# Two transformer layers and two hybrid layers on one core: where the steps of a norm, a group of loads and some weight splits are issued

## The chip, the core and the metric

The kernel runs on one NeuronCore of a Trainium2 chip. Five engines work side by side, each in the order of its own queue: TensorE (PE; its weight loads are shown as PEld), VectorE (DVE), ScalarE (ACT), GpSimd (POOL) and SyncE (SP), which here only issues DMAs. The metric is the device time of one execution in microseconds (us), lower is better. Times of the kernel before: 3697.65, 3699.57 and 3701.98 us, median 3699.57.

## The reference

A stream `x` of 512 tokens by 1024 features goes through two "first" layers and two "second" layers. Weights and activations are float32. What matters here:

```python
# first block, for l in 0, 1:
y = _group_rmsnorm(mix, mix_g[l]) @ w_o[l]             # mix: four attention groups
x = _layernorm(ALPHA * x + y, ln1_g[l], ln1_b[l])
f = (silu(x @ w_gate[l]) * (x @ w_up[l])) @ w_down[l]   # d_ff 2816
x = _layernorm(ALPHA * x + f, ln2_g[l], ln2_b[l])
# second block, for l in 0, 1:
x = x + 0.5 * swiglu(rms_norm(x, ffn_norm[l, 0]), ...)
x = x + mixers(rms_norm(x, mix_norm[l]) @ w_in[l]) @ w_out[l]
x = x + 0.5 * swiglu(rms_norm(x, ffn_norm[l, 1]), ...)
```

So there are six SwiGLU feed-forward blocks (called FFN 1 to 6 here, in order of time). FFN 1 and 2 follow the output projection of the attention layers, FFN 3 follows the down projection of FFN 2, FFN 4 follows the output projection of a mixer, FFN 5 follows the down projection of FFN 4, FFN 6 follows the output projection of the second mixer.

## The kernel before, in words

**Precision.** Every float32 operand is split into a high part (a cast to float32r on ACT) and a low part (a subtraction, mostly on DVE, every other output weight on POOL), and each product is three matmuls: high-high, low-high, high-low (`mm3`). A weight is loaded by `raw` (line 255, an SP DMA into one of three `wr` buffers), and split by `weight` (line 236: cast at line 250, subtraction at line 251).

**An FFN (`swiglu`, line 705).** The hidden width is 22 tiles of 128. The first four tiles are "early": they are computed as plain products from operands that don't need the finished norm. The other 18 go in pairs through `fast` (line 604), which computes a pair of tiles with seven half-size products in place of eight, from seven combinations of `x` made by `combos` (line 564). The hidden tiles are used in three chunks (8, 8 and 6 tiles; of these 4, 2 and 3 pairs come from `fast`), each followed by eight tiles of the down projection (`dn`).

**With `finish` (FFN 1, 2, 3).** The stream still has to be normalised. `early` (line 737) multiplies the un-normalised, gain-scaled stream (`psh`, `psl`, made by `presplit`) and `unfold` (line 487) repairs the result later. Meanwhile `lnrows` gets the statistics, and its rows (`lnr`, `lnb`) are there after the second product of early tile 0. `finish` is a generator of 18 steps: 10 of the layer norm (`ln`), then 8 of `combos` (two for each of four `k`). `steps(todo, n)` in the loop over early tiles issues the next `n` of them behind early tile `f`.

**Without `finish` (FFN 4, 5, 6).** The generator is `combos` alone, 8 steps (each `k` with two scalings by a gain), issued 2 at a time behind early tiles 0, 1, 2 and the rest behind tile 3.

**The seven-product loads.** `fast` loads quarters of a pair of gate or up tiles: `e` (from quarter c), `a`, `d` and `b`, 512 KB each, on SP (line 623); and on POOL (line 621) it adds quarter `d` into `e` and quarter `c` into `a` by an accumulating DMA from DRAM. `prep(j)` splits the operand of product `j`; products 0 to 6 use a, e, e+a, b, a+c, e+a+b, d. The buffers `wr2` (five) belong to a pool that takes the place of small tiles of the attention or mixer phase; `b` uses a `wr` buffer. `fast` is called three times in each FFN, 18 times in all.

**The output projection (`project`, line 329).** For each part of the mix that is ready it issues eight jobs of `wo` weights (128x256 each for a part of two tiles) through `dense` (line 265). `dense` splits weights `AHEAD` = 3 jobs ahead of use, or the first `head` of them at once, and then into ordinary slots in place of the three `wh`/`wl` buffers. Ahead of the last part, `heads` issues gate and up of early tile 0. `last` makes the split operands of the FFN from each finished tile of `x`, and `sums` adds up its sums and squares.

**What sets the order.** Nothing is ordered by hand. A list scheduler replays the program in its own model of the chip and gives each engine the instruction that is ready there, earliest in program order first; so a DMA whose buffer is free can be issued long before the place where it is written. `tc.issue_after(ins)` keeps the instructions that a block issues on the engine of `ins` behind `ins` in that engine's queue, without waiting for it to finish.

Of the kernel before, what the change touches and what calls it, by code (L numbers as in the profile page):

```python
# [19 lines left out]
KT = 8  # L20
# [17 lines left out]
LOOK = 2  # L38
MID = 0
FIN = 0  # L40
LSTEP = 5
NSTEP = 2
SLOTF = 1
PROJ1 = dict(w=(12, 13, 14, 15), s=(8, 10), S=(9, 11), a=(0, 1), b=(2,), f=(4, 6), F=(5, 7))
# [25 lines left out]
class Ctx:  # L70
# [183 lines left out]

    def raw(self, src, n, name):
        raw = self.wp.tile([128, 1024], F32, name=self.nm(name), tag="wr", bufs=NWR)[:, :n]
        self.nc.sync.dma_start(raw, src)
        return raw

    def mm3(self, acc, l, r, first, last):  # L260
# [68 lines left out]
    def project(self, E, src, xd, parts, scale, st, mean, last, wgu):  # L329

        nc = self.nc

        def add(n, j, ps):
            x = E["x"][j]
            if n == 0 and scale != 1.0:
                nc.vector.scalar_tensor_tensor(x, x, scale, ps, op0=OP.mult, op1=OP.add)
            else:
                nc.vector.tensor_add(x, x, ps)
            if n == len(parts) - 1:
                last(x, j)  # L340
                self.sums(st, x, j, mean)
        for n in range(len(parts)):
            yield "part%d" % (n + 1)
            if n == 0:
                E["x"] = self.refill(xd)
            k, ms = parts[E["parts"][n]]
            ms = ms()
            if n == len(parts) - 1:
                self.heads(wgu)
            w = src[:, :, k * 128:(k + len(ms)) * 128]  # L350
            yield from self.dense([self.tjob(w[j], len(ms), 128, ms, lambda ps, j=j: add(n, j, ps), None, "wo")
                                   for j in range(KT)])

    def gemm(self, acc, w, xs):
        for k, x in enumerate(xs):
# [59 lines left out]
    def rows(self, col, ps=None):  # L415

        n = col.shape[-1]
        ps = self.P("rowp")[:, :n * 128] if ps is None else ps
        for t in range(n):
            self.mm(ps[:, t * 128:t * 128 + 128], col[:, t:t + 1].to_broadcast([128, 128]), self.ident)  # L420
        return ps
# [182 lines left out]
    def fast(self, wgu, f0, n, cs, rows, put, between):  # L604


        nc = self.nc
        H = KT // 2
        quarter = {"a": (0, 0), "b": (0, 1), "c": (1, 0), "d": (1, 1)}
        raws, ws = {}, {}  # L610
        total = 7 * (n // 2)

        def tile_(pool, tag, bufs, dt=F32):
            return pool.tile([128, 1024], dt, name=self.nm("sw" + tag), tag=tag, bufs=bufs)

        def move(i, q, t, add=False):
            g, h = quarter[q]
            f = f0 + 2 * i
            src = wgu[g, f:f + 2, :, h * 512:h * 512 + 512].rearrange("f p c -> p f c")
            if add:  # L620
                nc.gpsimd.dma_start(t.rearrange("p (f c) -> p f c", f=2), src, accum_op=OP.add)  # L621
            else:
                nc.sync.dma_start(t.rearrange("p (f c) -> p f c", f=2), src)

        def load(i, q, src=None):
            raws[i, q] = tile_(self.wp, "wr", NWR) if q == "b" else tile_(self.fp, "wr2", NRAW)
            move(i, src or q, raws[i, q])

        def prep(j):
            i, s = divmod(j, 7)  # L630
            R = lambda q: raws[i, q]
            if s == 0:
                if i == 0:
                    load(0, "e", "c")
                    move(0, "d", R("e"), True)
                    load(0, "a")
                load(i, "d")
                load(i, "b")
            elif s == 2:
                nc.vector.tensor_add(R("e"), R("e"), R("a"))  # L640
            elif s == 5:
                nc.vector.tensor_add(R("e"), R("e"), R("b"))
                del raws[i, "b"]
            r = R("aeebaed"[s])
            hi, lo = (tile_(self.wp, "w" + t, NWS, F32R) for t in "hl")
            nc.scalar.copy(hi, r)  # L646
            nc.vector.tensor_sub(lo, r, hi.bitcast(F32))  # L647
            ws[j] = hi, lo
            if s == 2:
                move(i, "c", R("a"), True)  # L650
            if s == 4 and i + 1 < n // 2:
                load(i + 1, "e", "c")
                move(i + 1, "d", raws[i + 1, "e"], True)
                load(i + 1, "a")
            if s >= 4:
                del raws[i, "aed"[s - 4]]
        tags = ["s", "s", "o", "d"]
        bank = 0
        acc, g, u2 = {}, {}, {}
        for j in range(min(SAHEAD, total)):  # L660
            prep(j)
        for j in range(total):
            i, s = divmod(j, 7)
            if j + SAHEAD < total:
                prep(j + SAHEAD)
            between(j)
            hi, lo = ws.pop(j)
            fresh = s in (0, 1, 3)
            if fresh:
                tag = tags[bank % 4]  # L670
                bank += 1
                acc["AE0B"[s]] = [self.P("gup", tag)[:, 0:256] for _ in range(2)]
            a = acc["AEABAEA"[s]]
            for e in range(2):
                for k in range(H):
                    w = slice(e * 512 + k * 128, e * 512 + k * 128 + 128)
                    x, first, last = cs[s][k], fresh and k == 0, k == H - 1
                    self.mm(a[e], hi[:, w], x[0], first, False, not fresh)
                    self.mm(a[e], hi[:, w], x[1], False, False, not fresh)
                    self.mm(a[e], lo[:, w], x[0], False, last, not fresh)  # L680
            A, B = slice(0, 256), slice(256, 512)
            for e in range(2):
                if s == 0:
                    g[e] = self.S("gt")
                    nc.scalar.copy(g[e][:, A], a[e])
                elif s == 1:
                    if e == 0:
                        u = self.S("up")
                        u2 = {0: u[:, A], 1: u[:, B]}
                    nc.scalar.copy(u2[e], a[e])  # L690
                elif s == 2:
                    nc.scalar.copy(g[e][:, B], a[e])
                elif s == 3:
                    nc.vector.tensor_sub(g[e][:, A], a[e], g[e][:, A])
                elif s == 4:
                    nc.vector.tensor_add(u2[e], a[e], u2[e])
                elif s == 5:
                    nc.vector.scalar_tensor_tensor(g[e][:, B], a[e], -1.0, g[e][:, B], op0=OP.mult, op1=OP.subtract)
                    if rows() is not None:
                        nc.vector.tensor_mul(g[e], g[e], rows())  # L700
                    nc.scalar.activation(g[e], g[e], AF.Silu)
                else:
                    put(f0 + 2 * i + e, g[e], a[e], u2[e])

    def swiglu(self, xs, wgu, wdn, evac, stats, ahead, finish=None, npre=0, mix=None):
# [5 lines left out]
        ws, raw, h = dict(self.head), [], [None] * FT  # L711
# [17 lines left out]
        def products(f, xs):  # L729
            w = get(f, f + 1)  # L730
            gu = [self.P("gup", "s") for _ in range(2)]
            for i in range(2):
                self.gemm(gu[i], w[i], xs)
                tick()
            return gu

        def early(f, xs):
            w = get(f, f + LOOK)
            a, out = self.P("gup", "s"), []
            for i in range(2):  # L740
                b = self.P("gux", "do"[i])[:, 0:258]
                self.gemmx(a[:, i * 256:i * 256 + 256], b, w[i], xs)
                tick()
                out.append(self.unpack(a[:, i * 256:i * 256 + 256], b, "a", "gu"[i] + "r"))
            return out
# [21 lines left out]
        def steps(it, n):  # L767
            for _ in range(n):
                try:
                    next(it)  # L770
                except StopIteration as e:
                    return True, e.value
            return False, None
        todo = None if finish else mix(cs)
        for f in range(npre):
            if finish:
                raw.append(early(f, xs))
                if f == 1:
                    lnr = rows
                    todo = finish(lnr, cs)  # L780
            else:
                raw.append([(self.evac(ps, "a", name="gu"[i] + "r"), None) for i, ps in enumerate(products(f, xs))])
            if todo:
                end, v = steps(todo, 100 if f == npre - 1 else LSTEP if finish else 2)
                if end and finish:
                    stats, ticks = v, 0
        xs = None
# [1564 lines left out]
```

## Time and profile before

| | |
|---|---|
| median of three runs | 3699.57 us |
| the profiled execution, as timed | 3712.78 us |
| its span in the profile | 3711.0 us |
| PE busy | 3561.6 us, 96% of the span |
| PEld, DVE, ACT, POOL busy | 82%, 70%, 48%, 11% |
| mean granted TensorE clock | 0.978 of full speed |
| HBM traffic | 101 GB/s over the span |

A busy engine is one with an instruction in flight. Matmuls are pipelined, so PE at 96% doesn't mean that it does 96% of what it could: a lone matmul is shown longer than the interval at which matmuls follow each other. The number of matmuls in a stretch, set against a stretch in which they run without a break, tells more. The granted clock has two levels, 1.2 and 2.4 GHz; a share of a stretch between 0.5 and 1 means that it had some of each.

### The profile page before, as it was taken

To read this page: it belongs to the slowest core of one execution; us is meant where nothing else is said; L and a number is where in the kernel's file an instruction comes from. 1 tells how busy PE (TensorE), PEld (TensorE's weight loads), DVE (VectorE), ACT (ScalarE), POOL (GpSimd) and SP (SyncE) were. 2 spreads that over 40 slices of the span, in tenths; PEclk is the share of its full clock that TensorE was granted. 3 is DMA by queue.
4 is the path that set the end of the run, shared out by engine and by line. 5 is a ranking of instruction groups with operands and counts; after the bars stand their busy time and mean duration, and the time that the engine had idled before them with its cause. 6 is when DMAs were issued, how large, how long until landed. Compare 5 with 4: busy or idle time off the path is not lost.

```text
span 3711.0 us, 58410 instructions
## 1 busy us (share of the span) xinstructions
PE 3561.6 (96%) x22612; PEld 3059.9 (82%) x22612; DVE 2611.0 (70%) x5227; ACT 1772.7 (48%) x3392; POOL 422.7 (11%) x402
## 2 busy tenths in 40 slices
PE   9998999999899999999998999999999999799999
PEld 7677989776789988889776779898989777688888
DVE  5377766747676568767699667666867678957766
ACT  5464544646454346535443645435534533445433
POOL 1112000111200010001212011000000211100000
PEclk9999999999999999999998999999999999899999
DMA  3124543221434443544211245434643321223443
GB/s 129 48 66 113 139 129 89 100 66 49 125 91 135 121 133 86 132 128 137 82 55 42 69 120 143 130 97 119 160 120 95 102 70 51 80 69 108 131 123 94
DMA packets 196998, 377.94 MB, mean 102 GB/s; under 512 B 32456, under 2 KB 58728, under 8 KB 196464
## 3 DMA queue, kind: packets, MB, share of 16 engines
q1 hardware_dynamic: 167344, 317.57, 26.5%
q0 software_dynamic: 29376, 56.63, 9.7%
q8 instruction: 178, 2.92, 0.3%
q14 instruction: 100, 0.82, 0.1%
HBM read 358.36 MB, written 15.78 MB: 101 GB/s over the span
## 4 chain that ended last, share of the span: by engine, by line
PE 74%; DVE 16%; DMA 3%; ACT 3%; issue 3%; POOL 0%; ACTq 0%; POOLq 0%; DVEq 0%; SPq 0%
PE gup L179 25%; PE dn L179 19%; PE pjp L179 6%; PE tp L179 3%; PE wop L179 3%; PE sc L179 2%; DVE swwl L647 2%; PE gux L179 2%; PE ot L179 1%; DMA swwr<-in_w_gu_dram 1%; ACT swwh L646 1%; PE pt L183 1%; PE iY L179 1%; PE G L179 1%; PE iR L179 1%
## 5 line engine op out<-in xcount | busy, mean ns | idle before, releaser
L646 ACT CAST swwh<-swwr 128x1024 fp32r<-128x1024 f32 x378 | 395.0, 1051 | 510.5 <-PE gup L179 205.3
L647 DVE TENSOR_TENSOR swwl<-swwr,swwh 128x1024 fp32r<-128x1024 f32 x378 | 460.9, 1224 | 222.5 <-ACT swwh L646 214.3
L179 PE MATMUL gup<-cth,swwh 128*128 128x256 f32 x1728 | 487.4, 284 | 21.6 <-ACT cth L592 17.3
L179 PE MATMUL gup<-cth,swwl 128*128 128x256 f32 x1728 | 488.9, 283 | 2.3 <-DVE swwl L647 2.2
L179 PE MATMUL gup<-ctl,swwh 128*128 128x256 f32 x1728 | 489.2, 283 | 1.6 <-DVE ctl L597 1.6
L179 PE MATMUL dn<-hh,downl 128*128 128x512 f32 x1056 | 413.4, 394 | 1.4 <-DVE downl L251 1.4
L179 PE MATMUL dn<-hl,downh 128*128 128x512 f32 x1056 | 414.0, 394 | 0.1
L179 PE MATMUL dn<-hh,downh 128*128 128x512 f32 x1056 | 413.1, 395 | 0.0
L179 PEld LDWEIGHTS gup<-cth,swwh 128*128 128x128 f32 x1728 | 326.5, 190 | 25.9 <-ACT cth L592 20.6
L621 POOL DMA_DIRECT2D swwr<-in_w_gu_dram x108 | 130.0, 1203 | 1862.5 <-DVE swwr L640 1068.1
L179 PEld LDWEIGHTS gup<-ctl,swwh 128*128 128x128 f32 x1728 | 328.8, 190 | 3.8 <-DVE ctl L597 3.8
L179 PEld LDWEIGHTS gup<-cth,swwl 128*128 128x128 f32 x1728 | 328.6, 190 | 3.7 <-DVE swwl L647 3.7
L250 ACT CAST downh<-down 128x1024 fp32r<-128x1024 f32 (+1 forms) x144 | 141.0, 979 | 262.0 <-PE dn L179 177.7
L179 PE MATMUL gup<-cnl,swwh 128*128 128x256 f32 x864 | 244.6, 284 | 3.0 <-DVE cnl L594 3.0
L179 PE MATMUL gup<-cnh,swwh 128*128 128x256 f32 x864 | 242.3, 284 | 2.1 <-ACT cnh L581 2.1
L179 PE MATMUL gup<-cnh,swwl 128*128 128x256 f32 x864 | 243.5, 282 | 0.0
L179 PEld LDWEIGHTS dn<-hl,downh 128*128 128x128 f32 x1056 | 198.3, 188 | 48.0 <-DVE hl L229 3.2
L179 PEld LDWEIGHTS dn<-hh,downh 128*128 128x128 f32 x1056 | 198.0, 188 | 48.3 <-ACT hh L228 2.3
L179 PEld LDWEIGHTS dn<-hh,downl 128*128 128x128 f32 x1056 | 198.3, 188 | 47.8 <-DVE downl L251 1.9
L179 PE MATMUL pjp<-xsh,pjh 128*128 128x512 f32 x472 | 202.2, 429 | 14.2 <-ACT tpe L218 8.0
L179 PE MATMUL pjp<-xsl,pjh 128*128 128x512 f32 x472 | 194.7, 413 | 3.2 <-DVE xsl L535 3.1
L179 PE MATMUL pjp<-xsh,pjl 128*128 128x512 f32 x472 | 194.5, 412 | 0.0
(649 smaller groups left out, 8666.4 us busy)
## 6 DMA issues: line engine op xcount, KB each, us to landing
swwr<-in_w_gu_dram SPq DMA_DIRECT2D x216, 512.0 KB, 4.0
swwr<-in_w_gu_dram POOLq DMA_DIRECT2D x108, 512.0 KB, 6.2
down<-in_w_dn_dram SPq DMA_DIRECT2D x96, 512.0 KB, 3.7
pj<-in_w_in_dram SPq DMA_DIRECT2D x62, 512.0 KB, 3.6
down<-in_w_dn_dram SPq DMA_DIRECT2D x48, 384.0 KB, 3.1
wo<-in_w_o_dram SPq DMA_DIRECT2D x96, 128.0 KB, 2.2
g<-in_w_gu_dram SPq DMA_DIRECT2D x24, 512.0 KB, 3.7
u<-in_w_gu_dram SPq DMA_DIRECT2D x24, 512.0 KB, 4.1
```

Source lines behind the costliest of these rows:

```text
L179: self.nc.tensor.matmul(out, l, r, start=start, stop=stop, skip_group_check=more)
L183: self.nc.tensor.transpose(out, src, self.ident if ident is None else ident)
L250: nc.scalar.copy(hi, r)
L621: nc.gpsimd.dma_start(t.rearrange("p (f c) -> p f c", f=2), src, accum_op=OP.add)
L646: nc.scalar.copy(hi, r)
L647: nc.vector.tensor_sub(lo, r, hi.bitcast(F32))
```

## The change

Three things. The steps of `finish` begin behind early tile 0 in place of tile 1, in numbers 4, 8, 6, 0 (before: none, 5, 5, the remaining 8), and those of FFN 4 to 6 in numbers 2, 4, 2, 0 (before: 2, 2, 2, 2). The first loads of each call of `fast` (`e` and `a`) are queued on SP behind the last load that `raw` has issued by then: the last early weight in the first call, the last down weight in the other two. And the last part of each output projection splits its first six weights at once, into slots.

```diff
-LSTEP = 5
+PACEF = (4, 8, 6, 0)
+PACEN = (2, 4, 2, 0)
+HLAST = 6
@@ raw
-        self.nc.sync.dma_start(raw, src)
+        self.loaded = self.nc.sync.dma_start(raw, src).ins
@@ project
             yield from self.dense([self.tjob(w[j], len(ms), 128, ms, lambda ps, j=j: add(n, j, ps), None, "wo")
-                                   for j in range(KT)])
+                                   for j in range(KT)], HLAST if n == len(parts) - 1 else 0)
@@ fast, prep
                 if i == 0:
-                    load(0, "e", "c")
+                    with self.tc.issue_after(self.loaded):
+                        load(0, "e", "c")
+                        load(0, "a")
                     move(0, "d", R("e"), True)
-                    load(0, "a")
                 load(i, "d")
                 load(i, "b")
@@ swiglu
-                if f == 1:
+                if f == 0:
                     lnr = rows
                     todo = finish(lnr, cs)
@@ swiglu
-                end, v = steps(todo, 100 if f == npre - 1 else LSTEP if finish else 2)
+                end, v = steps(todo, 100 if f == npre - 1 else PACEF[f] if finish else PACEN[f])
```

## Rows read from the trace of the kernel before

**Rows 1.** The page: the span, and the chain that ended last by engine.

```profile
span 3711.0 us, 58410 instructions
PE 74%; DVE 16%; DMA 3%; ACT 3%; issue 3%; POOL 0%; ACTq 0%; POOLq 0%; DVEq 0%; SPq 0%
```

**Rows 2.** Waits of PE: who waited for whom: us in total, times, longest.

```profile
PE gup L179 <- ACT cth L592: 17.3, 14, 2.2
PE wop L179 <- ACT woh L250: 9.0, 3, 4.5
```

**Rows 3.** Busy us (x instructions) by engine, PEclk, DMA share, GB/s: starts of `fast`.

```profile
365.00:385.00 20.00, 12.29 (x64) 9.86 (x63) 18.08 (x41) 12.15 (x28) 0.33 (x1) 0.83 0.19 26
385.00:405.00 20.00, 20.00 (x171) 20.00 (x170) 14.42 (x21) 12.87 (x19) 2.39 (x2) 1.00 0.56 136
...
1425.00:1445.00 20.00, 12.90 (x64) 11.25 (x64) 19.59 (x56) 16.24 (x34) 0.00 (x0) 0.74 0.16 26
...
2231.00:2241.00 10.00, 9.38 (x72) 8.51 (x71) 8.28 (x14) 7.99 (x16) 0.00 (x0) 1.00 0.54 121
```

**Rows 4.** Timeline of FFN 1, ACT and DVE: start, us, engine, line, operation.

```profile
331.76 0.59 ACT L510 COPY lnr<-rowp 128x512 f32<-128x512 f32 x1 [7.96 <-PE rowp L179]
...
339.74 1.28 DVE L521 TENSOR_TENSOR lnt<-x,lnr 128x512 f32<-128x512 f32 x2
...
373.17 0.41 DVE L584 TENSOR_TENSOR ct<-x 128x256 f32<-128x256 f32 x1
...
383.22 0.68 DVE L597 TENSOR_TENSOR ctl<-cu,cth 128x512 fp32r<-128x512 f32 x1
```

**Rows 5.** Busy time as in rows 3: rows ready to first `fast` product, FFN 1, 3.

```profile
332.40:366.40 34.00, 33.61 (x277) 32.95 (x276) 21.65 (x35) 15.94 (x29) 1.20 (x1) 1.00 0.17 48
...
1388.90:1424.90 36.00, 35.99 (x299) 35.51 (x298) 25.84 (x43) 20.12 (x37) 1.20 (x1) 1.00 0.14 45
```

**Rows 6.** DVE groups by line in 332.4 to 366.4: count, busy us, mean ns, idle.

```profile
L492 DVE TENSOR_TENSOR gr<-gr,lnr 128x512 f32<-128x512 f32 x4 | 2.7, 684 | 3.6 <-ACT lnr L510 3.6
```

**Rows 7.** Busy time as in rows 3: the last part of FFN 1's projection.

```profile
285.00:289.00 4.00, 3.55 (x15) 2.18 (x14) 1.83 (x4) 0.96 (x3) 0.73 (x1) 1.00 1.05 351
...
293.50:298.00 4.50, 4.50 (x11) 3.38 (x12) 1.75 (x4) 1.87 (x7) 0.72 (x1) 0.50 0.77 166
```

**Rows 8.** Timeline of ACT in that stretch: the cast of FFN 1's first up weight.

```profile
292.28 0.62 ACT L250 CAST uh<-u 128x512 fp32r<-128x512 f32 x1 [2.70 <-DMA u<-in_w_gu_dram]
```

**Rows 9.** The chain, in order of time: start, us, what (FFN 1 twice, then FFN 4).

```profile
285.06 7.20 DMA u<-in_w_gu_dram
...
402.45 6.24 DMA swwr<-in_w_gu_dram
...
2160.00 5.27 DMA wo<-in_w_o_dram
```

**Rows 10.** DMA issues: queue, count, KB each, median us from issue to landing.

```profile
swwr<-in_w_gu_dram SPq DMA_DIRECT2D x216, 512.0 KB, 4.0
swwr<-in_w_gu_dram POOLq DMA_DIRECT2D x108, 512.0 KB, 6.2
...
wo<-in_w_o_dram SPq DMA_DIRECT2D x96, 128.0 KB, 2.2
...
u<-in_w_gu_dram SPq DMA_DIRECT2D x24, 512.0 KB, 4.1
```

**Rows 11.** SP's queue in FFN 1: last early weight; last five down weights of chunk one.

```profile
324.93 0.33 SPq L257 DMA_DIRECT2D u<-in_w_gu_dram  x1
...
455.98 17.39 SPq L257 DMA_DIRECT2D down<-in_w_dn_dram  x5
```

**Rows 12.** Timeline of PE: first product of FFN 1's second call of `fast`.

```profile
503.83 0.28 PE L179 MATMUL gup<-cnh,swwh 128*128 128x256 f32 x1
```

**Rows 13.** Tile views, projection of FFN 1: count, min/median/max ns, first and last start.

```profile
L484 DVE SCALAR_TENSOR_TENSOR psl<-x,vec,psh x8: 737/1207/1784, 299.7 to 321.8; 128x512 fp32r<-128x512 f32 x8
...
L251 POOL TENSOR_TENSOR wol<-wo,woh x7: 718/740/1283, 278.2 to 311.1; 128x256 fp32r<-128x256 f32 x7
```

## The prediction

> **What bounds the kernel now.** I read the page first, for who stands on the chain that ends last: TensorE has 74% of it, DVE 16%, DMA 3%, ACT 3% [rows 1]. So a gain must come from places where PE stands still. The waits of PE name two that this change touches: its products waiting for ACT's casts of the `combos` operands, 17.3 us in 14 waits, and the output projection waiting for ACT's weight casts, 9.0 us in 3 waits [rows 2]. Both figures are too small for what is lost, because a lone matmul is shown longer than its share of a running stream and because the clock falls. The count of matmuls tells more. In the 20 us at the start of FFN 1's `fast`, 64 matmuls run; in the next 20 us, at full clock, 171 [rows 3]. 64 at that rate take 7.5 us, so 12.5 us are lost, part of it as a granted clock of 0.83. FFN 2 repeats this. FFN 3 has 64 in 20 us at a clock of 0.74, the same 12.5 us [rows 3]. FFN 4 has 72 in 10 us where 85.5 would run, a loss of 1.6 us, and FFN 5 and 6 repeat that [rows 3].
>
> Then the timeline of the stretch before it. In FFN 1 the norm's rows are ready from 331.76 on, the first norm operation on DVE starts at 339.74, and the `combos` steps run until 383.22 + 0.68 = 383.90, well past the first `fast` product at 366.4 [rows 4]. Yet between the rows and that product DVE is busy for 21.65 of 34 us, ACT for 15.94, PE without a break [rows 5]. The work that PE waits for could have been done under the early tiles; it is issued too late.
>
> **Part 1, the steps of `finish`.** Nothing is added or removed: 18 steps move forward, the norm behind tile 0, the first `combos` behind tile 1, the other three behind tile 2. Three `combos` take from 373.17 to 383.90, 3.58 us each on DVE, 14.3 us for four [rows 4]. Of DVE's 21.65 us in the window, seven `unfold` multiplies of 0.684 us (four of them in rows 6; the other three are the same operation on `up`) are 4.8 us that are written behind `fast` and can go there. The need is 21.65 - 4.8 + 14.3 = 31.2 us of 34: it fits, with 2.8 us to spare for the ping-pong between ACT and DVE [rows 5, 6]. ACT has 18 us free. In front of what does this work move? On DVE and ACT, in front of the splits of early tile 3's weights, and only with the first `combos`, 3.6 us; as the queue there has free time, I cost that at nothing, and at up to 3.6 us of PE for an FFN if it does not. I take a rest of 2.5 us of the 12.5 and so a gain of **10 us each in FFN 1 and 2** (bounds 3 and 12.5).
>
> FFN 3 has more to do: the sums of the stream and a scaling of each half by a gain. DVE: 25.84 - 4.8 + 14.3 = 35.3 of 36 us; ACT has 20.12 us, and the four `combos`, which make up most of its 16.24 us in the 20 us after, come on top, some 15 us: 35 of 36 [rows 3, 5]. Both engines are full, so the last `combos` will be some us late. I take **8 us** (bounds 2 and 12.5).
>
> FFN 4 to 6: the last `combos` moves from tile 3 to tile 2. I take 1 us of the 1.6 each, **3 us** (bounds -2, if a step delays a weight split, and 4.8).
>
> **What is late next.** With PE on time, the accumulation of quarter c into `a` follows product 2's sum and must land before product 4: a POOL DMA has a median of 6.2 us to landing [rows 10], and one stands on the chain already, 6.24 us, in FFN 1's second pair [rows 9]. In the first pair it was hidden behind the late `combos`. I give back **1.5 us in each of FFN 1 to 3, -4.5 us** (bounds 0 and -9).
>
> **Part 2, the queue of the `fast` loads.** Moved are two SP loads of 512 KB in each of 18 calls, and with the first of them POOL's accumulation into it. In FFN 1 they and what follows them are now issued inside the last part of the output projection. From 285 to 289 us the DMA engines are full, 351 GB/s [rows 7]. The first up weight, issued at 285.06, takes 7.20 us where 4.1 is the median [rows 9, 10]; ACT's queue stands behind its cast for 2.70 us [rows 8], with the output weight that PE waits for behind it; and the following 4.5 us run at a clock of 0.50 with 11 matmuls [rows 7]. Those take 0.235 us each in a full-rate stream (two of the 256-column ones of rows 3), 2.6 us, so 1.9 us go there. Gain 3.1 + 1.9 = 5.0, of which I take 4.5 in FFN 1; FFN 2 repeats the pattern with a wait one us longer, 5.0. In FFN 4 an output weight of 128 KB takes 5.27 us for a median of 2.2 [rows 9, 10], 3.1 us, and FFN 6 repeats it; 2.5 each, because the mixer's own end lies close behind. FFN 3, where down weights stand in place of output weights: 1. **Together 15.5 us** (bounds 0, if other loads of `fast` take the place of those held back, and 20).
>
> What it costs: the loads come later. In FFN 1's first call they now follow 324.93 [rows 11]; a load (4.0), an accumulation (6.2) and the splits of about 3 us are done by 340, for a product at 366. In the second call the last of the down weights is issued at 455.98 + 17.39 = 473.4 [rows 11], done by 487, for a product at 503.83 [rows 12]. 16 us and more are left, so nothing, in all 18. On POOL the moved accumulation passes the projection's sums and splits, which then start earlier, if anything.
>
> **Part 3, six weights at once.** Of the last eight output weights the splits of the fourth to sixth move ahead of the evictions of the first three jobs, with three loads of 128 KB. The same instructions run, two on POOL of 0.74 us at the median [rows 13] and one on DVE, and PE is bounded there by DVE's chain of sums and operand splits. I take 0 (bounds -2, as the first evictions come later, and 2 in each of four places).
>
> A rule bears on that. On the row: the operand split `psl` takes 0.737 us at least and 1.784 at most, 1.207 at the median [rows 13], in the stretch where POOL works on `x` and on these splits. The Trainium skill, page "SBUF — State Buffer", section "Who interferes with whom", says that a DVE instruction with two SBUF inputs and a GpSimd instruction that reads SBUF lock each other out, one waiting for the other in full. By that, two POOL splits moved out of DVE's busiest stretch would free up to 2 x 1.0 us of DVE in each of four projections, and the sum below would be 8 us better. The rows show long and short cases but not which partner made them long, so the sum goes without it.
>
> **The sum.** 10 + 10 + 8 + 3 - 4.5 + 15.5 + 0 = 42 us. The profiled execution (span 3711.0, 3712.78 with what lies around it) would become 3670.8; it is 13.2 us above the median of the runs, so against 3699.57 I forecast 3657.6, rounded to **3658 us**.
>
> **Rivals.**
> (a) The steps start earlier but the last `combos` still ends after the first product, since ACT and DVE hand each other work and the free time comes in pieces too short. For it: DVE is at 92% of the window in FFN 1 by my count and at 98% in FFN 3. Against it: before, the steps ran on DVE almost without a gap. Half of the 28 us of FFN 1 to 3: 3672 us. Chance 0.15.
> (b) The gate holds only `e` and `a`; `d` and the next pair's loads are free to go early and fill the DMA engines as before. Part 2 is then worth nothing: 3673 us. Chance 0.10.
> (c) Slower: the gate. Twelve of the 18 calls follow a chunk of the down projection, where the loads now come behind its last weight. If that weight's load is pushed back in the queue by more than the 16 us of margin, each us beyond costs PE a us, at each of twelve places. To end over 0.2% (7.4 us) slower with 42 us gained, it takes 49/12 = 4.1 us at each: loads 20 us later than now. At 5 us each, 42 - 60 = -18: 3718 us. Chance 0.07, as the down weights are paced by their three buffers and not by these loads.
> (d) It doesn't do what it says: the scheduler issues by readiness, and the norm's first steps wait for something other than their place in the program. Then parts 1 and 2 leave PE's waits as they are: 3700 us. Against it: the rows are ready 8 us before the first norm step, with DVE idle. Chance 0.07.
> (e) All of it, with the lock of DVE and POOL eased as well: 3640 us. Chance 0.03.
> The forecast itself: 0.58.
>
> **How the numbers follow.** Runs can tell a difference of about 0.2%, 7.4 us. Faster by more: forecast, a, b and e, 0.86; within: d, 0.07; slower: c, 0.07. For the range, the poor ends taken together (3 us each in FFN 1 and 2, 2 in FFN 3, 1 in FFN 4 to 6, half of part 2, less the 4.5) give a gain of 12 us, 3687; of the upper ones 12.5 x 3 + 4.8 + 20 = 62 us, 3637. From 3637 to 3687 holds the forecast and a, b, e, some 0.83 with what lies beyond the ends; c and d are left out.
>
> **What would show it.** Right, part 1: in the 20 us after FFN 1's first `fast` product some 150 matmuls, no clock below 0.9, `combos` finished on DVE within 2 us of that product; in FFN 3 some 125. Part 2: no load of `fast` on SP between FFN 1's output weights, first up weight down in about 4 us, projection and early tiles 4 to 5 us shorter. Wrong: `combos` still running 10 us after the first product; PE idle inside the early tiles for `gl` or `ul`; a wait for a `fast` load at the start of a second or third call.

## The result, and the profile after

The changed kernel takes 3664.95 us (median of 4 runs, 3659.73 to 3666.47) against 3700.78 for the kernel before (4 runs, 3697.65 to 3705.63): ratio 0.990, 95% interval 0.9882 to 0.9917, 35.8 us less. Its profiled execution took 3665.83 us. That of before, on which the prediction's rows rest, took 3712.78, 12 us over its median. So a second profile of before was taken, the **control** below, and differences of traces are taken against that.

The page after: span, chain by engine, the `fast` loads (KB each, median us to landing).

```profile
span 3664.1 us, 58412 instructions
PE 76%; DVE 15%; issue 3%; ACT 3%; DMA 2%; POOL 0%; ACTq 0%; DVEq 0%; POOLq 0%
swwr<-in_w_gu_dram SPq DMA_DIRECT2D x216, 512.0 KB, 5.4
```

The waits of PE after that answer [rows 2]: us in total, times, longest.

```profile
PE gup L181 <- ACT cth L594: 5.1, 5, 1.5
...
PE gup L181 <- ACT gr L211: 2.1, 3, 0.7
...
PE wop L181 <- ACT woh L252: 1.1, 4, 0.3
```

Both waits that the change aims at are much smaller, 17.3 to 5.1 and 9.0 to 1.1. A new one has come: PE waits 2.1 us for `gr`, ACT's evictions (copies out of the accumulator `gup` that PE has filled) of an early tile's gate product; the control's list has no such wait. The held loads now come five in a row, and the median of all 216 loads is 5.4 us instead of 4.0 [rows 10].

Busy time by window after, columns as in [rows 3] (PE, PEld, DVE, ACT, POOL, then PEclk, DMA share, GB/s): FFN 1 from the rows to the first `fast` product, the 20 us behind that product and the next 20; then the 20 us behind FFN 3's first product and the 10 us behind FFN 4's.

```profile
321.30:352.00 30.70, 30.70 (x259) 30.54 (x258) 27.20 (x52) 20.13 (x38) 1.21 (x1) 1.00 0.48 126
352.00:372.00 20.00, 16.32 (x112) 14.92 (x112) 14.03 (x27) 10.30 (x21) 1.20 (x1) 0.91 0.29 57
372.00:392.00 20.00, 20.00 (x172) 19.96 (x171) 14.31 (x20) 10.28 (x16) 2.39 (x2) 1.00 0.63 141
1386.90:1406.90 20.00, 14.78 (x71) 12.19 (x71) 16.78 (x48) 11.74 (x24) 1.20 (x1) 0.74 0.17 26
2191.00:2201.00 10.00, 10.00 (x86) 9.96 (x85) 5.14 (x5) 6.61 (x11) 0.87 (x1) 1.00 0.57 118
```

Against [rows 3], FFN 1 has 112 matmuls where 64 stood (full rate: 172), FFN 4 is at full rate with 86 for 72, and FFN 3 has hardly moved: 71 for 64, at the same clock of 0.74. The count has a catch: 24 of the 112 and 24 of the 71 are no products of `fast` but one half of early tile 3's `up` product, which before ran in front of it. Timeline of ACT and PE, FFN 1 and FFN 3:

```profile
359.94 0.36 ACT L211 COPY gr<-gup 128x256 f32<-128x256 f32 x1
360.36 0.58 PE L181 MATMUL gup<-psh,uh 128*128 128x256 f32 x1 [0.64 <-ACT gr L211]
...
1398.73 0.36 ACT L211 COPY gr<-gup 128x256 f32<-128x256 f32 x1
1399.14 0.58 PE L181 MATMUL gup<-psh,uh 128*128 128x256 f32 x1 [0.68 <-ACT gr L211]
```

These matmuls go into the accumulator that the tile's gate product fills, and wait for its eviction; ACT does that behind the last casts of the `combos`. They start 8.4 us (FFN 1) and 12.2 us (FFN 3) behind `fast`'s first product. In FFN 3, where PE had run 39 matmuls in the 12 us before, all 24 follow each other every 0.213 us at a granted clock of 0.50 (the lower level), against 0.117 us at full rate. So the first product comes earlier against its rows partly because work that stood in front of it now stands behind.

Timeline of FFN 1 after, ACT and DVE (answers [rows 4]): start, us, engine, line, operation.

```profile
321.27 0.58 ACT L512 COPY lnr<-rowp 128x512 f32<-128x512 f32 x1 [7.97 <-PE rowp L181]
...
322.49 1.28 DVE L523 TENSOR_TENSOR lnt<-x,lnr 128x512 f32<-128x512 f32 x2
...
343.92 1.05 ACT L649 CAST swwh<-swwr 128x1024 fp32r<-128x1024 f32 x1 [2.81 <-PE gup L181]
344.87 0.37 ACT L211 COPY ur<-gup 128x256 f32<-128x256 f32 x1
345.14 0.42 ACT L583 ACTIVATE cnh<-x 128x256 fp32r<-128x256 f32 x1
...
359.08 0.68 DVE L599 TENSOR_TENSOR ctl<-cu,cth 128x512 fp32r<-128x512 f32 x1
```

The norm begins 1.2 us behind the rows (from the start of ACT's copy), not 8. But the `combos` end at 359.08 + 0.68 = 359.8, still 7.8 us behind the first product at 352.0 (17.5 before). The second `combos` (345.14) follows at once on the eviction of early tile 2 (`ur`, 344.87), before which ACT had stood idle for 2.81 us: that is the place behind which it was written.

The last part of FFN 1's projection: after in two windows, and the control at the same point of the work in three (columns as above).

```profile
277.00:282.00 5.00, 4.65 (x21) 3.45 (x20) 5.00 (x10) 3.00 (x6) 1.28 (x1) 1.00 0.62 174
282.00:287.00 5.00, 3.69 (x14) 2.18 (x13) 4.04 (x6) 2.11 (x6) 0.93 (x1) 1.00 0.30 107
```

```profile
275.00:280.00 5.00, 4.55 (x19) 3.11 (x18) 3.53 (x7) 1.43 (x4) 0.17 (x1) 1.00 1.07 297
280.00:285.00 5.00, 1.74 (x6) 0.78 (x5) 2.58 (x5) 1.88 (x4) 1.78 (x2) 0.98 1.01 324
285.00:290.00 5.00, 4.71 (x14) 3.47 (x15) 2.54 (x5) 2.27 (x8) 1.03 (x1) 0.68 0.80 170
```

The full DMA engines of [rows 7] are there in the control (324 GB/s, 6 matmuls in 5 us, then a clock of 0.68) and gone after (107 GB/s, 14 matmuls, clock 1.00).

### The profile page after: what moved, and what is told of

Its sections match the earlier page's. It is cut to its first block, busy times and chain, and to the rows that moved or that the text cites. A ratio compares the mean times of both kernels' runs of the same rounds, so it can differ in the third digit from the quotient of the medians.

```text
span 3664.1 us, 58412 instructions
## 1 busy us (share of the span) xinstructions
PE 3538.9 (97%) x22612; PEld 3049.0 (83%) x22612; DVE 2616.5 (71%) x5227; ACT 1772.2 (48%) x3392; POOL 423.6 (12%) x402
## 4 chain that ended last, share of the span: by engine, by line
PE 76%; DVE 15%; issue 3%; ACT 3%; DMA 2%; POOL 0%; ACTq 0%; DVEq 0%; POOLq 0%
PE gup L181 26%; PE dn L181 19%; PE pjp L181 7%; PE wop L181 4%; PE tp L181 3%; PE sc L181 2%; DVE swwl L650 2%; PE ot L181 1%; PE gux L181 1%; DMA swwr<-in_w_gu_dram 1%; PE pt L185 1%; ACT swwh L649 1%; PE iY L181 1%; PE iR L181 1%; PE G L181 1%
```

## A ruler for the traces

For each FFN I measured one stretch: from the first matmul of its output projection to the first matmul of `fast`'s second pair of tiles (for FFN 4 and 6 from the first matmul of the projection's second part, as the first part lies inside the mixer and ends some 67 us earlier; for FFN 3 and 5, which have no projection, from the end of the FFN before). The late matmuls of early tiles lie inside it, so it holds the same work in every version but those that leave something out. It leaves out the mixers and the held loads of `fast`'s second and third calls; from its end to the end of the FFN, control and after differ by at most 1.7 us, and by 0.1 in the sum of the six. The two profiles of before differ by up to 1.1 us in a stretch and by 2.8 us in the sum: so much is scatter. In us, from the traces; the last columns are the sum of the six differences from the control, and the runs: ratio with its interval, times 3701.

| kernel | FFN 1 | FFN 2 | FFN 3 | FFN 4 | FFN 5 | FFN 6 | sum | runs |
|---|---|---|---|---|---|---|---|---|
| control | 177.6 | 178.3 | 88.0 | 124.1 | 69.0 | 121.3 | | |
| after | 166.7 | 166.2 | 85.8 | 119.0 | 66.4 | 118.5 | -35.7 | 0.9900 (-31 to -44) |
| steps alone | 170.0 | 169.1 | 86.9 | 121.6 | 67.9 | 118.9 | -23.9 | 0.9940 (-17 to -28) |
| loads held, alone | 174.1 | 172.2 | 85.5 | 121.0 | 68.1 | 119.7 | -17.7 | 0.9954 (-11 to -23) |
| six weights alone | 171.7 | 171.7 | 87.3 | 122.3 | 69.6 | 120.8 | -14.9 | 0.9972 (-6 to -16) |
| steps + held | 168.7 | 167.1 | 85.8 | 119.2 | 66.4 | 118.2 | -32.9 | 0.9916 (-25 to -37) |
| steps + six weights | 167.1 | 166.1 | 87.8 | 119.2 | 69.7 | 118.1 | -30.3 | 0.9908 (-28 to -40) |
| steps behind tile 1 | 165.8 | 166.7 | 85.3 | 119.5 | 66.2 | 119.1 | -35.7 | 0.9905 (-28 to -42) |
| behind tile 0 | 169.9 | 170.7 | 85.8 | 124.5 | 68.0 | 121.8 | -17.6 | 0.9948 (-13 to -26) |
| behind 0 and 1 | 165.9 | 164.7 | 82.8 | 120.1 | 66.3 | 118.3 | -40.2 | 0.9891 (-34 to -47) |
| after, no low parts | 162.6 | 166.9 | 83.8 | 120.3 | 66.4 | 119.3 | -39.0 | 0.9900 (-31 to -43) |
| behind 0 and 1, no low parts | 159.2 | 158.3 | 81.3 | 119.7 | 66.4 | 118.2 | -55.2 | 0.9849 (-50 to -61) |
| behind 0 and 1, low on POOL | 180.6 | 178.7 | 92.8 | 120.5 | 66.4 | 118.0 | -1.3 | 1.0007 (-1 to +6) |

Every sum lies within its interval or 0.3 us beside it: within what the runs can tell, these stretches hold the effect.

## The experiments

**The control**: the kernel before, unchanged.

> The kernel before, unchanged, profiled beside the other runs. The profiled execution of before that the prediction rests on (3712.78 us) lies 12 us above the median of that kernel's runs, that of after (3665.83) at the median of its own (3664.95), so the two traces differ by 46.9 us where the runs differ by 35.8. If that profile was only a long execution, this one will take about 3700 us, and the landmarks of the six FFNs will show where the 12 us lay. If profiling this kernel always costs it 12 us (its waits on transfers being lengthened by the profiler's own traffic), this one will take 3710 or more.

```profile
core 0: 3696.3 us, clock 0.981
```

The core's span and mean clock: 3698.02 us for the execution, near the median of the runs, so it is not the profiling that costs 12 us; the first profile was a long execution. Its surplus in span, 14.8 us, lies elsewhere: 3.3 us of it are there by the load of `wv` at 92 us, 7.9 by that of `uq` at 142, both in the first mixer. The rest comes and goes in later mixers and FFNs, by 1 to 3 us at a time. The stretches of the ruler agree within 1.1 us between the two.

**Each part alone.** First the steps (the places of the change, with the loads and output weights of before):

```
+PACEF = (4, 8, 6, 0)
+PACEN = (2, 4, 2, 0)
...
-                if f == 1:
+                if f == 0:
```

> Part 1 alone: the steps of the norm, the combos and the stream's sums at their new places, with the loads of fast and the output weights as before. Theory A (the prediction): 26.5 us gained, ratio 0.993; the end of FFN 1's first pair of tiles comes 8.5 us earlier, FFN 2 another 8.5, FFN 3 6.5, FFN 4 to 6 together 3. Theory B (read from the two traces): the steps carry 6 us of FFN 1, where the last early weight's load alone came 10.5 us earlier, 3.5 us in FFN 3, and 8 in FFN 4 to 6. Theory C: the two parts need each other, because the splits of the late early weights stand in front of the steps: alone under 15 us, ratio above 0.996.

3679.14 us, 0.994. Theory A is close: 7.6 and 9.2 us in FFN 1 and 2 for 8.5 each, 6.0 in FFN 4 to 6 for 3, but 1.1 in FFN 3 for 6.5, no more than the scatter of a stretch. C falls.

Then the hold of the loads:

```
+                    with self.tc.issue_after(self.loaded):
+                        load(0, "e", "c")
+                        load(0, "a")
                     move(0, "d", R("e"), True)
-                    load(0, "a")
```

> Part 2 alone: the loads of fast behind the last load before the call, steps and output weights as before. Theory A: 15.5 us gained, ratio 0.9958; FFN 1's early tiles start 4.5 us earlier, FFN 2's another 5. Theory B: the last early weight comes 10 us earlier on SP in FFN 1 as in after, and the early tiles begin 5 us earlier, but what lies between is not gained where the combos steps stay late. Rival: nothing, as d and the next pair take the place in the DMA engines (ratio 1.000).

3685.28 us, 0.9954: 17 us for the 15.5 of theory A. In FFN 1 the gain lies inside the projection, as the prediction put it: 90.8 us from its first to its last matmul for 94.3.

Then the six weights:

```
-                                   for j in range(KT)])
+                                   for j in range(KT)], HLAST if n == len(parts) - 1 else 0)
```

> Part 3 alone: six output weights split ahead in the last part of the projection, all else as before. Theory A: 0 us (bounds -2 and +2 in each of four places), ratio 1.000. Rival, the lock of DVE and POOL: 8 us gained, 0.998. Rival, the six weights hold slots of the memory that the fast loads take over, so it holds these loads back as the gate does: 4 to 10 us gained, with the first fast load on SP in FFN 1 later than the 279.6 us or so of the kernel before.

3689.91 us, 0.9972, 10 us gained where the prediction had 0. SP's queue tells why: the first `fast` loads of FFN 1, in four fences the control, the held loads alone, the six weights alone, and after; a fifth has a line of SP's waits (us, times, longest) with the six weights alone, in 262 to 303 us.

```profile
264.83 0.89 SPq L623 DMA_DIRECT2D swwr<-in_w_gu_dram  x2
```

```profile
312.63 2.51 SPq L625 DMA_DIRECT2D swwr<-in_w_gu_dram  x5
```

```profile
292.35 0.43 SPq L625 DMA_DIRECT2D swwr<-in_w_gu_dram  x1
301.05 0.94 SPq L625 DMA_DIRECT2D swwr<-in_w_gu_dram  x2
```

```profile
314.81 2.53 SPq L625 DMA_DIRECT2D swwr<-in_w_gu_dram  x5
```

```profile
SPq L625 <- PE wop L181: 0.3, 1, 0.3
```

The six weights alone hold the loads back by 27 us. By the code, their split halves take tiles of the mixer's memory (`slots`, 256 columns), and `fast`'s raw weights are put where that memory was; in the trace, the wait in the fifth fence is one of a `fast` load on SP for the output projection's matmuls. So part 3 was a second hold, and part 2 one that lasts longer. That the hold is all of its gain is not shown: see the pairs.

**The parts in pairs.**

```
-HLAST = 6
+HLAST = 0
```

> Parts 1 and 2 without part 3 (HLAST 0). The gate alone gave 0.9954 and the six weights alone 0.9972, and in the latter no load of fast stood between FFN 1's last output weights and the first came at 292.35 where the kernel before has 264.83. If the two do the same thing, holding those loads back, this one equals after, ratio 0.990 within 0.001. If the six weights bring a gain of their own (the lock of DVE and POOL), it is 8 to 10 us slower than after, ratio 0.9925. If they only cost once the gate holds the loads (as 0.994 x 0.9954 = 0.9894 and after's own 0.990 would allow), it is 2 us faster than after.

> Parts 1 and 3 without part 2 (no hold on the loads of fast but what the six weights bring). Steps alone gave 0.994, steps with the hold 0.9916, all three 0.990. If holding the loads by either part is the same, this equals after, 0.990, within 0.001. If the explicit hold is worth something of its own in FFN 2 to 6, 0.992 to 0.993.

Steps and hold: 3667.32 us, 0.9916. Steps and six weights: 3667.02, 0.9908. All three: 0.990. The three intervals overlap, so either hold does most of what both do; whether the second is worth its 2 to 6 us is not settled. With the loads held, the six weights go with a projection of 88.7 us for 92.1 in FFN 1 and 89.0 for 90.3 in FFN 2 (after against steps and hold), one trace each. In the ruler the explicit hold brings 5.3 us in FFN 3 and 5 (after against steps + six weights), which the six weights can't reach, as no projection stands before these.

**Where the rest of the stall in `fast` comes from.** After part 1 the `combos` still end 7.8 us (FFN 1) and 11.3 us (FFN 3) too late. Is it their place, or is DVE full?

```
-PACEF = (4, 8, 6, 0)
-PACEN = (2, 4, 2, 0)
+PACEF = (4, 14, 0, 0)
+PACEN = (4, 4, 0, 0)
```

> The kernel after, with all combos steps begun behind early tile 1 (PACEF (4, 14, 0, 0), PACEN (4, 4, 0, 0)). In after, ACT's first operation of the second combos starts 0.26 us behind the last eviction of early tile 2 in FFN 1 (345.14, eviction 344.87) and in FFN 3 (1384.64, 1384.38), while ACT stood idle before. Theory P (place): steps issued behind a tile begin when that tile's evictions are planned, so their place and not the engines' time holds them. Then the combos end some 8 us earlier in FFN 1 to 3, before the first fast product; 3 to 4 us gained in FFN 1 and 2 each, 6 to 7 in FFN 3 (which shows 79 matmuls in 1385 to 1405 at a clock of 0.74): about 14 us, 3651 us, ratio 0.986 to before. Rival S (saturation, the prediction's case a): DVE and ACT are full under the early tiles, and the combos end where they do in after: 3665, ratio 0.990.

3662.61 us, 0.9905. The `combos` now end 33.6 us behind the rows (38.5 in after), so the place did hold them; yet the 14 us of theory P did not come, and PE has gained nothing that the runs can tell. In its trace 48 matmuls of early tiles, not 24, come behind `fast`'s first product in each of FFN 1 to 3. Next, everything behind tile 0:

> All steps behind early tile 0 (PACEF (18, 0, 0, 0), PACEN (8, 0, 0, 0)). Theory P: no more than the version behind tile 1, if there the combos already end before the first product; the steps now stand ahead of the weight splits of tiles 2 and 3 as well, 14 us of DVE, so PE can run dry of weights inside the early tiles: 3650 to 3665. Rival S: the early tiles starve, PE's gaps in them grow to 10 us in each FFN: 3680 or more.

3681.16 us, 0.9948, 16 us worse than after, as rival S had it. Waits of PE in 330 to 350 us, then in a second fence windows (columns as above) inside the early tiles and behind the first product:

```profile
PE gup L181 <- ACT gr L211: 7.3, 1, 7.3
```

```profile
338.50:358.50 20.00, 12.66 (x89) 12.05 (x89) 13.88 (x33) 9.58 (x22) 0.00 (x0) 0.83 0.11 32
362.50:382.50 20.00, 20.00 (x172) 20.00 (x171) 12.55 (x18) 12.51 (x19) 1.53 (x2) 1.00 0.68 153
```

Now `fast` starts at full rate, 172 matmuls, but the early tiles stop for 7.3 us: PE waits for ACT's eviction `gr`, which ACT does at 345.60, straight behind the last `combos` cast (345.08). The stall has changed places; the wait is of the same kind as the one that holds the 24 matmuls in after. Between the two:

> Between the two: the first three combos steps begun behind tile 0, the rest behind tile 1 (PACEF (10, 8, 0, 0), PACEN (2, 6, 0, 0)). Theory P: as the version behind tile 1 to within 3 us, 3648 to 3654; FFN 4 to 6 within 1 us of it. Rival S: as after, 3665.

3659.83 us, 0.9891, the fastest that leaves nothing out; its median is 5 us below after's, but the intervals overlap, and it lies between the figures of both theories. PE no longer waits for `cth` at all, but 3.3 us for `ur` and, in the list of its waits,

```profile
PE gup L181 <- ACT gr L211: 3.9, 3, 1.3
```

with 48 matmuls of early tiles behind the first product. To see DVE's share, its subtractions for the low parts of the weights of early tiles 1 to 3 are left out in FFN 1 to 3 (a part of the edit):

```
-            (eng or nc.vector).tensor_sub(lo, r, hi.bitcast(F32))
+            if eng != "hi":
+                (eng or nc.vector).tensor_sub(lo, r, hi.bitcast(F32))
```

> The kernel after, with DVE's subtraction for the low parts of the weights of early tiles 1 to 3 left out in FFN 1 to 3 (the high part stands in for the low one, so those tiles are computed wrongly; ACT, PE and the loads do the same work). It takes six DVE operations of 1.216 us, 7.3 us, from each of the three FFNs. In after DVE is busy 32.3 of the 35 us before the combos end in FFN 1. Theory D (DVE's work over the whole stretch is the bound, and the places of the steps only shift where PE waits for it): the combos end 5 to 7 us earlier and each FFN gains 4 to 6 us, 12 to 18 in all, 3647 to 3653. Rival L (what counts is only the order on DVE and the handing to and fro with ACT): the combos end within 2 us of where they do in after, and under 5 us are gained in all, 3660 or more.

On the places of after: 3659.81 us, 0.990, the same ratio as after. The `combos` take as long behind the rows as before, 39.6 us for 38.5, as rival L had it. FFN 1 gains 4.1 us in the ruler, but FFN 2 nothing, and the sum only 3.3. Theory D doesn't hold there.

> The version with the steps behind tiles 0 and 1 (3659.8 us), with DVE's low parts of the weights of early tiles 1 to 3 left out in FFN 1 to 3 as in the earlier run (those tiles are computed wrongly). In after the same omission moved the combos' end against the rows not at all (38.5 us from the rows to their end, 39.6 without the subtractions), because the second combos starts behind tile 2's evictions there; here it starts 3.5 us behind the first. Theory D with P (once the place no longer holds them, DVE's work does): the combos end 3 to 6 us earlier against the rows than the 33.1 us of the version, and 3 to 4 us are gained in each FFN, 3648 to 3651. Rival (PE's remaining stall has nothing to do with the amount of DVE's work): 3656 to 3660.

On the better places the same omission brings 3647.25 us, 0.9849, 12.6 us less than with the subtractions. FFN 1: rows to the end of the `combos` with the subtractions and without (columns as above), then without them the 20 us behind the first product in FFN 1 and FFN 3.

```profile
317.60:350.70 33.10, 31.12 (x258) 30.54 (x256) 31.26 (x63) 21.97 (x41) 2.44 (x2) 1.00 0.51 132
```

```profile
315.30:344.70 29.40, 29.40 (x248) 29.23 (x247) 26.79 (x60) 22.01 (x43) 1.21 (x1) 1.00 0.49 119
...
344.80:364.80 20.00, 20.00 (x170) 19.89 (x169) 13.78 (x19) 9.32 (x18) 1.20 (x1) 1.00 0.33 79
1364.50:1384.50 20.00, 14.69 (x93) 13.69 (x92) 16.31 (x39) 11.19 (x26) 1.20 (x1) 0.74 0.18 26
```

DVE was busy 31.26 of 33.1 us; with those subtractions gone the `combos` end with the first product, and PE goes on at full rate, 170 matmuls. 48 of them are early ones that now start 0.2 us behind the first product, where with the subtractions they start 5.8 us behind it. The omission also spares PE the wait for the low parts, but that is not the gain: counted from the start of the projection the first product comes at 133.4 us for 133.9, and the 6.7 us of FFN 1 lie behind it. So both answers hold in FFN 1 and 2, one behind the other: in after the place of the second `combos` holds the chain; with a better place DVE's work holds the `combos` and, behind their casts, ACT's evictions. FFN 3 stays late even so (93 matmuls, clock 0.74): the `combos` end 38.0 us behind the end of the rows' copy for 38.6, and only 1.5 us went. What holds it there is open.

Last, can POOL take the subtractions, being idle there?

```
-        return [self.weight(wgu[i, f], KT, 128, "gu"[i], None, f < SLOTF) for i in range(2)]
+        return [self.weight(wgu[i, f], KT, 128, "gu"[i], self.nc.gpsimd if f >= SLOTF and self.fin else None, f < SLOTF) for i in range(2)]
```

> The version with the steps behind tiles 0 and 1 (PACEF (10, 8, 0, 0), 3659.8 us), with the same six subtractions moved from DVE to POOL, which has 2.4 us of work in the 35 us before FFN 1's combos end. POOL takes 2.43 us for one of this size where it splits the projection's weights. Theory D: up to 7.3 us less on DVE in each of FFN 1 to 3, less what DVE and POOL cost each other (a DVE subtraction of this size takes 1.215 us alone and 2.0 us beside POOL's work in FFN 1's projection): 2 to 4 us gained in each, 3648 to 3654. Rival L: nothing, 3660. Rival P: POOL's 2.43 us, behind its waits for loads and accumulations in its queue, come too late for PE and cost 2 to 5 us in each: 3666 to 3675.

3700.52 us, 1.0007: 40 us lost against the same kernel with them on DVE, far outside all three forecasts. Timeline of POOL and of DVE in FFN 1, then the one wait of PE in 340 to 380 us:

```profile
334.94 5.10 POOL L253 TENSOR_TENSOR ul<-u,uh 128x1024 fp32r<-128x1024 f32 x1 [9.53 <-ACT uh L252]
341.08 2.41 POOL L253 TENSOR_TENSOR gl<-g,gh 128x1024 fp32r<-128x1024 f32 x1 [1.04 <-ACT gh L252]
347.40 14.19 POOL L253 TENSOR_TENSOR ul<-u,uh 128x1024 fp32r<-128x1024 f32 x1 [3.91 <-ACT uh L252]
...
337.83 2.76 DVE L494 TENSOR_TENSOR ur<-ur,lnr 128x512 f32<-128x512 f32 x1
...
341.30 2.74 DVE L494 TENSOR_TENSOR ur<-ur,lnr 128x512 f32<-128x512 f32 x1
...
358.71 0.68 DVE L599 TENSOR_TENSOR ctl<-cu,cth 128x512 fp32r<-128x512 f32 x1
...
359.38 2.76 DVE L494 TENSOR_TENSOR gr<-gr,lnr 128x512 f32<-128x512 f32 x1
```

```profile
PE gux L181 <- POOL ul L253: 8.4, 1, 8.4
```

One subtraction that takes 2.41 us took 14.19, while DVE worked through its `combos` at normal length. Three multiplies of DVE took 2.74 to 2.76 us for 0.68, one beside each subtraction of POOL, and each ends 0.55 us behind it (361.59 and 362.14 for the last). PE waited 8.4 us for the last low part. That is about half of the 14.7 us that FFN 1 loses in the ruler (180.6 for 165.9); the other half, 7.5 us, is there before the rows are. Rival P had the sign, but by lateness in the queue; the rows show the two engines holding each other up.

## Why the prediction was right, and where it was off

Forecast 3658 us, measured 3665: 35.8 of 42 us gained, inside a wide range. By stages of the ruler, forecast against measured: FFN 1 13 and 10.9, FFN 2 13.5 and 12.1, FFN 3 7.5 and 2.2, FFN 4 3.5 and 5.1, FFN 5 1 and 2.6, FFN 6 3.5 and 2.8.

- **What bounds.** Right: the two waits were the ones to go, and in the kernel before, counting matmuls against the full rate sized them well. After the change the same window holds early matmuls too, so the count no longer compares.
- **Part 1, FFN 1 and 2.** 7.6 and 9.2 us for 8.5, but with some luck. The gross 10 us did not come: the `combos` ended 7.8 us late, and 112 matmuls ran, 24 of them early ones, where some 150 were named as the sign. The -1.5 us for late accumulations, which did not come either, made up for part of that. The count of DVE's work fitted with 2.8 us to spare only because the 4.8 us of `unfold` multiplies were taken out. Six of the seven, 4.1 us, still ran before the last `combos`: 31.2 + 4.1 = 35.3 us where 34 were there, and DVE was busy for 34.9 us from the rows to that point.
- **Part 1, FFN 3.** Here the same step of the prediction failed outright. It counted DVE at 35.3 of 36 us with the `unfold` multiplies taken out, as they are written behind `fast`. DVE's groups after, from the end of the rows' copy to the last `combos` (1354.3 to 1398.2), have six of them:

```profile
L494 DVE TENSOR_TENSOR gr<-gr,lnr 128x512 f32<-128x512 f32 x3 | 2.1, 685 | 6.1 <-ACT lnr L512 6.1
L494 DVE TENSOR_TENSOR ur<-ur,lnr 128x512 f32<-128x512 f32 x3 | 2.0, 683 | 0.0
```

  35.3 + 4.1 = 39.4 us, and DVE's busy time in that stretch of 43.9 us is 39.4. That doesn't fit in 36. A second term was put at nothing: in front of what the steps move. The prediction named weight splits; it was ACT's evictions of early tile 3, and with them 24 matmuls at half clock behind the first product. So the `combos` ended 10.8 us earlier from the start of the FFN than in the control, and steps alone brought 1.1 us for 8 less 1.5. Rival (a) had the late `combos`, but not the reason: where all steps stand behind tile 0, DVE is busy 31.9 of the 32.4 us from the end of the rows' copy to the last `combos` of this FFN, so handing work to and fro with ACT does not keep it idle. How the missing us divide between the two terms is not shown.
- **Part 1, FFN 4 to 6.** 1 us each was small: 2.5, 1.1 and 2.4 with the steps alone. The `combos` end 3.3 us before the first product, 7.1 behind it in the control, and no early matmul is left behind.
- **What is late next.** The 4.5 us given back for late accumulations did not show. PE waits for splits and not for loads, so its list of waits can't tell; but in the two versions where the `combos` were on time in FFN 1, PE ran through the first pair without a break (172 and 170 matmuls in 20 us). Late next were the `combos` themselves and ACT's evictions. Without that term part 1 stood at 28 us in FFN 1 to 3, against 17.9 measured with the steps alone: a cost that did not come hid 4.5 of the 10.1 us missing.
- **Part 2.** Right in size (17 us for 15.5) and place. Rival (b) falls: `d` and the next pair's loads stand behind `e` and `a` in SP's queue, and five came in a row at 312.63. The sign came too: the first up weight lands in 3.41 us after, for 7.48 in the control. Rival (c) falls: the first product of each second and third call starts 0.23 or 0.24 us behind the start of the last down matmul, in all twelve places, in the control as in the held version.
- **Part 3.** Forecast 0, alone 10 us. The prediction costed the instructions and three loads, but not the memory that, by the code, the six weights keep. Beside the hold of part 2 it is worth 2.8 us in the ruler and nothing that the runs settle, so the sum didn't suffer: 0 was nearly right in the whole change, for a reason not seen.
- **The rule on DVE and POOL.** `psl` fell from 1.208 us at the median (control) to 0.742 (after); in FFN 1's projection its eight take 8.5 us for 10.0. With the loads held alone it is 0.981 and 8.7, with the six weights alone, which hold the loads as well, 0.745 and 8.5. On top of steps and hold the six weights take the eight from 8.8 to 8.5 us, so what the moved splits themselves bring is small. The Trainium skill, page "SBUF — State Buffer", section "Who interferes with whom", told the direction; the 2 us for each of four places did not come. Where it bites is the POOL run above: there the trace agrees, in both directions.
- **The offset.** Right: the profile's surplus of 13 us was scatter, over half of it in the first mixer.

## What to carry to other kernels

Size a stall by counting matmuls against the full rate, and look which products they belong to when an edit may have changed their order. Ask of each step you move what it will stand behind and what will stand behind it, evictions too, and of each buffer you take early who wants its memory next: both were worth more here than the cost of the instructions. Work that is written later does not leave a window by that, if it is ready: take it out of a count only when something holds it back. When an engine comes out at 95% or more of the window it must fit, forecast the poor end. And measure all variants on the same stretches of work: two profiles of one kernel agreed within 3 us there, where their spans differed by 15.

## What the hardware showed that was not expected

- POOL's subtraction of 128x1024 took 2.41 us, 5.10 and 14.19 in one kernel, the last beside DVE's dense run of two-input operations; from the rows on, DVE's operations kept their length but for one multiply beside each, 2.74 to 2.76 us for 0.68. POOL looked free here, and was not for this work beside a full DVE.
- Two profiles of one kernel differed by 14.8 us in span, 7.9 of them in the first mixer, which none of these edits touches.
